# Twelve projection pieces and four gate pieces moved beside the second attention of a hybrid encoder layer; masks loaded later; the merge's PSUM pools kept and its buffers enlarged

## The chip, the cores and the metric

The kernel runs on one core of a Trainium2 chip. The core has a matrix engine (TensorE, in the profile PE, with its weight loads as PEld), VectorE (DVE), ScalarE (ACT), GpSimd (POOL), and SyncE (SP), which in this kernel only issues transfers (DMA). Each engine works through its own list of instructions in order and waits on semaphores for the others. Matrix products land in PSUM, eight banks of 128 x 512 float32; everything else is in SBUF, and larger intermediates go to DRAM and come back. The metric is the device time in microseconds (us), the median of several runs.

## What is computed

One layer of a bidirectional encoder, 2048 tokens of width 1024, float32. The tokens are also a grid of 32 rows by 64 columns.

```python
h = rms_norm(x, norm_mix)
z = h @ w_in              # q_A k_A v_A | q_B k_B v_B | gate_A gate_B
y_a = windowed_gqa(q_a, k_a, v_a, sink)       # 8 heads, |t - s| <= 128, ALiBi, sink logit
y_b = neighborhood_attn(q_b, k_b, v_b, rpb)   # 8 heads, 8 x 16 neighbours, learned bias
gates = sigmoid(concat([g_a, g_b]) + b_gate)
merged = gates[:, :D] * (y_a @ w_proj_a) + gates[:, D:] * (y_b @ w_proj_b)
x = x + merged @ w_out
x = x + square(relu(rms_norm(x, norm_mlp) @ w_up)) @ w_down
out = rms_norm(x, norm_final)
```

Every large product is made of three: each factor is split into a high and a low part (`mm3`, lines 190 to 193: high x high, high x low, low x high). So one product of 128 x 1024 by 1024 x 512 is 24 matmuls.

## The kernel before

The tokens are four blocks (`b`) of 512. The stages, with the line numbers of the profile:

1. *Input projections of blocks 0 and 1* (`in_quad`, Strassen-like, lines 412 to 438), up to line 561.
2. *Stage A, windowed attention* (`attn_a`, lines 624 to 681): 32 units, two groups of four heads times 16 blocks of 128 queries. A unit loads q, k and v (SP, lines 630 to 643), makes scores S (lines 649 and 650, PSUM tag `s`), adds the bias and takes the maximum on DVE (651), exponentiates on ACT (658), normalises on POOL (662); in its second half it transposes (668, PSUM `pt`), copies on ACT (671), subtracts on DVE (672) and multiplies with the values, PV (673 and 674, PSUM `av`). `done` collects each unit's last PV.
3. *Stage B, neighbourhood attention* (`attn_b`, lines 773 to 842): 32 units, eight heads times four column strips, in the same manner: S in line 795, maximum 799, exponential 805, normalising 809; transposes 821, copy 826, subtraction 827, PV 832. It loads qb (780 to 782), vb (786), kb (770, one per head), and for three of the four strips a bias table (763), to which POOL adds the masks (764). The masks are one tile of 128 x 3200 float32, loaded in line 747. Results go to DRAM as `y_b` through ACT's queue (`put` and `flush`).
4. *Merge* (lines 1121 to 1171): per block, products of the pages of `y_a` and `y_b` with `w_pa` and `w_pb` (PSUM `mm` and `s`), gates loaded from DRAM (`z<-zg`, 1134), sigmoid (1135), product, sum on POOL (1138), split (1139 and 1140), the product with `w_out` (PSUM `pt`), the norm, and transposes into `av` (1166). `load_y` (869 to 887) brings `y_a` and `y_b` back (`yraw`, 877) and splits them into pages.
5. *MLP*: up (from line 1180) and down (to the end), Strassen-like.

What matters here is the dense work that runs beside the attention. The input projections of blocks 2 and 3 aren't made in stage 1: `dense` (lines 722 to 727) is a list of 18 weight slices of 128 columns, k and v of A, four of q_A, and for each pair of B's heads `t` one each of k, q and v (KB, QB, VB). Each slice (`slice_of`) is a load of 512 KB, a split on ACT and POOL, and two pieces of 24 matmuls (PSUM `mm`), one for each block. The projections are stored to DRAM on SP's queue (595 and 608), in 2, 4 or 2 transfers a piece for KB, QB and VB. `gate_tile` does the same for the 16 gate slices, 32 pieces, and stores them on ACT's queue (719). So before the change 36 pieces run in stage A, and 32 gate pieces from stage B on.

The order on each engine is not written by hand: a scheduler places the instructions, with the program's order as priority. The attention stands first in the program; the dense pieces (`paced`) come after it and fill what it leaves. `paced` holds a piece back until a certain unit's PV is done:

```python
at = n * 32 // (total - rest) - lag if n < total - rest else 31
with tc.issue_after(done[at]) if at >= 0 else nullcontext():
    next(filler, None)
```

With `paced(fill, range(32), 32, 4, 4)` (line 890) the last four gate pieces wait for the last unit of B. `drive` (693 to 702) keeps two units between a unit's first half (S) and its second (PV).

Each transfer takes one of eight semaphores in turn, and its issuing engine waits until the transfer that had this semaphore before has landed.

Of the kernel before, what the change touches and what calls it, by code (L numbers as in the profile page):

```python
# [8 lines left out]
F32 = mybir.dt.float32  # L9
# [3 lines left out]
PSUM = bass.MemoryType.PSUM  # L13
# [9 lines left out]
P = 128  # L23
KC = D // P
NB = 4
# [65 lines left out]
def encoder_layer(ctx, tc, x, norm_mix, w_in, b_gate, sink, rpb, w_pa, w_pb, w_out,  # L91
# [529 lines left out]

    done = []

    def attn_a(g, i):
# [4 lines left out]
        q = T(ap_, [P, 4, P], F32R, "qa", 3)  # L629
        SY.dma_start(q.bitcast(F32), qs_a[g][i // 8][:, i % 8])  # L630
        ka = T(ap_, [P, 2, 384], F32R, "ka", 3)
# [51 lines left out]
    def chain(gens):  # L683

        now = None
        for g in gens:
            next(g)
            if now is not None:
                yield from now
            now = g  # L690
        yield from now

    def drive(units, ahead=2):

        live = []
        for u in units:
            next(u)
            live.append(u)
            if len(live) > ahead:
                next(live.pop(0), None)  # L700
        for u in live:
            next(u, None)

    def paced(filler, pieces, total, rest, lag):

        for n in pieces:
            at = n * 32 // (total - rest) - lag if n < total - rest else 31
            with tc.issue_after(done[at]) if at >= 0 else nullcontext():
                next(filler, None)

    def gate_tile(f, blocks):
        hl = slice_of([(cols(w_in[0], O_GA + f * P), KC)])
        yield
        for b in blocks:
# [5 lines left out]
            yield  # L720

    dense = [qk_tile(O_KA, 1.0), v_tile(O_VA)]
    dense += [qk_tile(O_QA + t * P, 0.125) for t in range(4)]
    for t in range(4):
        dense.append(qk_tile(O_KB + t * P, 0.125))
        dense.append(qk_tile(O_QB + t * P, 1.0, tiled=True))
        dense.append(v_tile(O_VB + t * P))
    fill = chain(dense)
    for g in range(2):
        make_bias_a(g)  # L730

    drive(attn_a(g, i) for g in range(2) for i in range(7))
    paced(fill, range(12), 36, 0, 3)
    flush()
    drive(attn_a(g, i) for g in range(2) for i in range(7, 16))
    paced(fill, range(12, 36), 36, 0, 3)
    del done[:]
# [8 lines left out]
    masks = T(bp, [P, btotal], F32, "masks", 1)  # L746
    SY.dma_start(masks, mask_b)
    jstart = {0: bstart[0], 1: bstart[2], 2: bstart[4]}
# [4 lines left out]
    def make_bias_b(h, jt):  # L753
        j = (0, 1, 3)[jt]
        w = B_W[j]
        n_bias[0] += 1
        t = T(bp, [P, 1280], F32, f"biasb{n_bias[0] % 2}", 2)
        for i in (0, 1, 3):
            n = B_NR[i] * w
            o = boff[(jt, IT[i])]  # L760
            first = h * T_ROWS * w + (B_R0[i] - 8 * i - 7 + T_RO) * w + (B_C0[j] - 16 * j - 15 + T_COFF[j])
            src = bass.AP(tabs[jt].tensor, tabs[jt].offset + first, [[w, 8], [1, 16], [1, n]])
            SY.dma_start(t[:, o : o + n], src)
        G.tensor_tensor(out=t[:, : jlen[jt]], in0=t[:, : jlen[jt]],
                        in1=masks[:, jstart[jt] : jstart[jt] + jlen[jt]], op=ALU.add)
        return t
# [94 lines left out]

    fill = chain(gate_tile(f, (2, 3)) for f in range(16))
    drive(ahead_of(all_b(), 1))
    flush()
# [4 lines left out]
    def load_y(b):  # L869
        yh, yl = [], []  # L870
        for n in range(2):
            h = T(p4, [P, 4, BT], F32R, "page", 4)
            l = T(p4, [P, 4, BT], F32R, "page", 4)
            for c in range(4):
                raw = T(p4, [P, BT], F32, "yraw", 2)
                src = (y_a[c // 2][(c % 2) * P : (c % 2 + 1) * P] if n == 0 else y_b[c])[:, b * BT : (b + 1) * BT]
                SY.dma_start(raw, src)
                hc, lc = h[:, c], l[:, c]
                if n == 1:

                    raw = flipped(raw)
                    hc, lc = (t.rearrange("p (r j c) -> p j r c", r=8, j=4) for t in (hc, lc))
                A.copy(hc, raw)
                V.tensor_tensor(out=lc, in0=raw, in1=hc.bitcast(F32), op=ALU.subtract)
            yh.append(h)
            yl.append(l)
        return yh, yl

    first_y = load_y(0)
    paced(fill, range(32), 32, 4, 4)  # L890
    s_h.close()

# [6 lines left out]
    wo = []  # L899

    s_pp.close()
    s_pp = ExitStack()
    pps.update({t: pool(f"pq_{t}", space=PSUM, stack=s_pp) for t in ("mm", "s", "pt", "av")})

# [217 lines left out]
    for b in range(NB):  # L1122
# [3 lines left out]
        for f in range(8):  # L1126
            hl = slice_of([(cols(w_pa[0], f * P), 4), (cols(w_pb[0], f * P), 4)])
            parts = []
            for n in range(2):
                ps = psum("mm" if n == 0 else "s", 2)  # L1130
                for c in range(4):
                    mm3(ps, hl[:, 0, 4 * n + c, :], hl[:, 1, 4 * n + c, :], yh[n][:, c], yl[n][:, c], c == 0, c == 3)
                g = T(wp, [P, 2, BT], F32, "z", 2)[:, 0] if n else T(p4, [P, BT], F32, "z", 2)
                SY.dma_start(g, zg[b][0][n, f * P : (f + 1) * P, :])
                A.activation(g, g, AF.Sigmoid, bias=bg[:, 8 * n + f : 8 * n + f + 1])
                V.tensor_tensor(out=g, in0=ps, in1=g, op=ALU.mult)
                parts.append(g)
# [25 lines left out]
        for k in range(KC):  # L1163
            ps = psum("av", 2)
            for t in range(4):
# [216 lines left out]
```

## Time and profile before

| | |
|---|---|
| median of 3 runs | 2761.67 us (2759.82 to 2764.2) |
| the profiled execution by itself | 2763.62 us |
| its span, first to last instruction | 2761.7 us |
| mean granted TensorE clock | 0.985 |
| busy PE | 2664.5 us, 96% of the span |
| busy DVE, ACT, POOL | 1561.0, 1244.9, 820.4 us |
| read from and written to DRAM | 342.94 and 155.26 MB |

The profile is one execution. Its page gives busy time by engine, the span in 40 slices (a digit is the busy share in tenths), the DMA queues, the chain of work that ended last, and groups of instructions by line. Views of the same trace give busy time by windows, the waits, the rows of one tile, and the instructions in order of time. A row of the latter reads: start, duration, engine, line, operation, written tile <- read tiles, and in brackets the idle time before it with what ended it. "SPq" and "ACTq" are the queues' issues of transfers. A matmul's duration overlaps the next one's.

### The profile page before, as it was taken

The numbers are of one execution on the slowest core, as the hardware profiler recorded it, in microseconds if no ns is written. First come the engines' busy times: TensorE is split into PE (matmuls) and PEld (weight loads), VectorE is DVE, ScalarE is ACT, GpSimd is POOL, SyncE is SP. The second block draws the span as 40 slices with busy tenths as digits, with TensorE's granted clock in tenths as the row PEclk, the third lists the DMA queues.
The fourth block names the chain that finished last, engine by engine and source line by source line (L and its number), as shares of the span: only waits on it lengthen the run. The fifth ranks groups of instructions, "written<-read, shape, count | busy, mean of one in ns | idle before, by whom it ended". The sixth has DMA issues, their size and how long they took to land.

```text
span 2761.7 us, 35569 instructions
## 1 busy us (share of the span) xinstructions
PE 2664.5 (96%) x12332; PEld 2196.4 (80%) x12332; DVE 1561.0 (57%) x2352; ACT 1244.9 (45%) x2227; POOL 820.4 (30%) x620
## 2 busy tenths in 40 slices
PE   7999989999989998999999999989999999999998
PEld 6887878888777787777878788878888788888887
DVE  8655455656355455533435767586654644555667
ACT  5334235555455456434433544554444332332444
POOL 1111133333354442423421355555544000000000
PEclk9999999999999998999999999999999999999999
DMA  4855276865677775646544656564434954445455
GB/s 147 229 152 190 101 230 191 221 184 158 171 205 203 202 189 157 200 131 201 181 144 171 237 167 210 186 219 149 150 137 160 331 180 160 141 153 179 171 190 173
DMA packets 348996, 500.58 MB, mean 181 GB/s; under 512 B 32505, under 2 KB 180601, under 8 KB 347665
## 3 DMA queue, kind: packets, MB, share of 16 engines
q1 hardware_dynamic: 319888, 464.74, 54.1%
q10 hardware_dynamic: 28928, 33.56, 3.6%
q8 instruction: 98, 1.61, 0.2%
q14 instruction: 82, 0.66, 0.1%
HBM read 342.94 MB, written 155.26 MB: 180 GB/s over the span
## 4 chain that ended last, share of the span: by engine, by line
PE 77%; DMA 10%; DVE 6%; issue 3%; ACT 2%; SPq 1%; POOL 0%; ACTq 0%; POOLq 0%; DVEq 0%
PE b L237 14%; PE b L239 14%; PE b L238 14%; PE mm L191 4%; PE mm L192 4%; PE mm L193 4%; PE zb L239 3%; PE zb L237 3%; PE zb L238 3%; DMA vb<-vs_b 3%; DMA z<-zg 2%; PE pt L191 1%; PE pt L192 1%; PE pt L193 1%; PE pt L668 1%
## 5 line engine op out<-in xcount | busy, mean ns | idle before, releaser
L238 PE MATMUL b<-dwh,dah 128*128 128x512 f32 x896 | 348.8, 389 | 0.0
L239 PE MATMUL b<-dwh,dah 128*128 128x512 f32 x896 | 348.0, 389 | 0.0
L237 PE MATMUL b<-dwh,dah 128*128 128x512 f32 x896 | 339.3, 391 | 2.2 <-ACT dwh L233 2.2
L230 POOL TENSOR_TENSOR uc<-uc,uc 128x512 f32<-128x512 f32 x120 | 233.5, 1961 | 221.1 <-issue 135.3
L233 ACT CAST dah<-da 128x1024 fp32r<-128x1024 f32 (+1 forms) x128 | 121.0, 945 | 366.5 <-PE b L239 243.7
L234 DVE TENSOR_TENSOR dah<-da,dah 128x1024 fp32r<-128x1024 f32 (+1 forms) x128 | 139.3, 1090 | 225.5 <-ACT dah L233 222.5
L237 PE MATMUL b<-ubh,uwhlb 128*128 128x512 f32 x592 | 231.3, 391 | 3.3 <-ACT uc L1077 1.6
L239 PE MATMUL b<-ubh,uwhlb 128*128 128x512 f32 x592 | 230.1, 391 | 2.7 <-DVE uwhlb L234 2.6
L238 PE MATMUL b<-ubh,uwhlb 128*128 128x512 f32 x592 | 231.1, 391 | 0.0
L191 PE MATMUL mm<-hT,whl 128*128 128x512 f32 x544 | 221.6, 407 | 2.3 <-DVE z L365 2.3
L230 DVE TENSOR_TENSOR uc<-b,uc 128x512 f32<-128x512 f32 x160 | 109.0, 688 | 196.4 <-PE b L239 153.4
L193 PE MATMUL mm<-hT,whl 128*128 128x512 f32 x544 | 216.8, 399 | 0.0
L192 PE MATMUL mm<-hT,whl 128*128 128x512 f32 x544 | 216.5, 398 | 0.0
L174 POOL TENSOR_TENSOR whl<-raw,whl 128x1024 fp32r<-128x1024 f32 x66 | 160.1, 2425 | 172.4 <-ACT whl L173 152.4
L237 PEld LDWEIGHTS b<-dwh,dah 128*128 128x128 f32 x896 | 168.8, 189 | 37.6 <-ACT dwh L233 2.6
L1272 POOL TENSOR_TENSOR st<-st,power 128x1 f32<-128x1 f32 x16 | 13.6, 859 | 616.0 <-DVE st L1271 615.8
L238 PEld LDWEIGHTS b<-dwh,dah 128*128 128x128 f32 x896 | 168.5, 188 | 35.0
L239 PEld LDWEIGHTS b<-dwh,dah 128*128 128x128 f32 x896 | 168.4, 188 | 35.0
L237 PE MATMUL zb<-zh,zwhl 128*128 128x512 f32 x476 | 189.8, 401 | 4.8 <-DVE zh L444 2.6
L238 PE MATMUL zb<-zh,zwhl 128*128 128x512 f32 x476 | 189.7, 399 | 1.8 <-DVE zh L234 1.8
L239 PE MATMUL zb<-zh,zwhl 128*128 128x512 f32 x476 | 187.0, 399 | 0.5 <-DVE zwhl L234 0.5
L237 PEld LDWEIGHTS b<-ubh,uwhlb 128*128 128x128 f32 x592 | 111.5, 188 | 27.1 <-ACT uc L1077 2.0
(236 smaller groups left out, 6232.4 us busy)
## 6 DMA issues: line engine op xcount, KB each, us to landing
at<-uc SPq DMA_DIRECT2D x224, 256.0 KB
da<-at SPq DMA_DIRECT2D x96, 512.0 KB
dw<-in_w_down_dram SPq DMA_DIRECT2D x160, 256.0 KB
uraw<-in_w_up_dram SPq DMA_DIRECT2D x32, 1024.0 KB
raw<-in_w_in_dram SPq DMA_DIRECT2D x34, 512.0 KB
zraw<-in_w_in_dram SPq DMA_DIRECT2D x16, 1024.0 KB
z<-zg SPq DMA_DIRECT2D x64, 256.0 KB
xin<-in_x_dram SPq DMA_DIRECT2D x16, 512.0 KB
```

The costliest lines, as they stand in the source:

```text
L174: G.tensor_tensor(out=hl[:, 1], in0=raw, in1=hl[:, 0].bitcast(F32), op=ALU.subtract)
L191: PE.matmul(ps, lh, rh, start=first, stop=False)
L192: PE.matmul(ps, lh, rl, start=False, stop=False)
L193: PE.matmul(ps, ll, rh, start=False, stop=last)
L230: return eng.tensor_tensor(out=out, in0=a, in1=b, op=op).ins
L233: A.copy(hi, src)
L234: eng.tensor_tensor(out=lo, in0=src, in1=hi.bitcast(F32), op=ALU.subtract)
L237: PE.matmul(ps, lh, rh, start=first, stop=False, skip_group_check=True)
L238: PE.matmul(ps, lh, rl, start=False, stop=False, skip_group_check=True)
L239: PE.matmul(ps, ll, rh, start=False, stop=last, skip_group_check=True)
L668: PE.transpose(pt[:, h * P : (h + 1) * P], s[:, h, c * P : (c + 1) * P], ident)
L1272: G.tensor_tensor(out=r, in0=r, in1=power, op=ALU.pow)
```

## The change

1. `dense` now runs in stage A only with its first 24 pieces (k, v, q of A, and heads 0 to 3 of B), paced over A's 32 units. The other 12 pieces (heads 4 to 7 of B) are put ahead of the 32 gate pieces in one chain, and these 44 are paced over B's 32 units, in two parts: 22 behind the first 15 units in the program's order, 22 behind the rest. The argument `rest` is gone, so that no piece is kept for after B.
2. `drive` takes its list of live units from outside and drains it only where `last` is true, so that the units of both parts are one stream.
3. `began` collects the first load of each unit of A. The load of the masks, and all loads of bias tables, are issued only after the 21st of them.
4. The merge keeps the PSUM pools of the attention instead of closing them and opening its own. `s` has three banks there instead of two, and the transposes behind the norm use one bank of `av` instead of two (in the last block three of `s`).
5. `yraw` has six buffers instead of two, the first gate tile `z` four instead of two.

```diff
-    done = []
+    done, began = [], []
...
-        SY.dma_start(q.bitcast(F32), qs_a[g][i // 8][:, i % 8])
+        began.append(SY.dma_start(q.bitcast(F32), qs_a[g][i // 8][:, i % 8]).ins)
...
-    def drive(units, ahead=2):
-
-        live = []
+    def drive(units, live, last, ahead=2):
+
         for u in units:
             next(u)
             live.append(u)
             if len(live) > ahead:
                 next(live.pop(0), None)
-        for u in live:
-            next(u, None)
-
-    def paced(filler, pieces, total, rest, lag):
+        while last and live:
+            next(live.pop(0), None)
+
+    def paced(filler, pieces, total, lag):
 
         for n in pieces:
-            at = n * 32 // (total - rest) - lag if n < total - rest else 31
+            at = n * 32 // total - lag
             with tc.issue_after(done[at]) if at >= 0 else nullcontext():
                 next(filler, None)
...
-    fill = chain(dense)
+    fill = chain(dense + [gate_tile(f, (2, 3)) for f in range(16)])
...
-    drive(attn_a(g, i) for g in range(2) for i in range(7))
-    paced(fill, range(12), 36, 0, 3)
+    live = []
+    drive((attn_a(g, i) for g in range(2) for i in range(7)), live, False)
+    paced(fill, range(12), 24, 3)
     flush()
-    drive(attn_a(g, i) for g in range(2) for i in range(7, 16))
-    paced(fill, range(12, 36), 36, 0, 3)
+    drive((attn_a(g, i) for g in range(2) for i in range(7, 16)), live, True)
+    paced(fill, range(12, 24), 24, 3)
...
-    SY.dma_start(masks, mask_b)
+    with tc.issue_after(began[20]):
+        SY.dma_start(masks, mask_b)
...
-            SY.dma_start(t[:, o : o + n], src)
+            with tc.issue_after(began[20]):
+                SY.dma_start(t[:, o : o + n], src)
...
-    fill = chain(gate_tile(f, (2, 3)) for f in range(16))
-    drive(ahead_of(all_b(), 1))
+
+    units = ahead_of(all_b(), 1)
+    drive((next(units) for _ in range(15)), live, False)
+    paced(fill, range(22), 44, 4)
+    flush()
+    drive(units, live, True)
...
-                raw = T(p4, [P, BT], F32, "yraw", 2)
+                raw = T(p4, [P, BT], F32, "yraw", 6)
...
-    paced(fill, range(32), 32, 4, 4)
+    paced(fill, range(22, 44), 44, 4)
...
-    s_pp.close()
-    s_pp = ExitStack()
-    pps.update({t: pool(f"pq_{t}", space=PSUM, stack=s_pp) for t in ("mm", "s", "pt", "av")})
...
-                ps = psum("mm" if n == 0 else "s", 2)
+                ps = psum("mm" if n == 0 else "s", 2 if n == 0 else 3)
...
-                g = T(wp, [P, 2, BT], F32, "z", 2)[:, 0] if n else T(p4, [P, BT], F32, "z", 2)
+                g = T(wp, [P, 2, BT], F32, "z", 2)[:, 0] if n else T(p4, [P, BT], F32, "z", 4)
...
-            ps = psum("av", 2)
+            ps = psum("av", 1) if b < NB - 1 else psum("s", 3)
```

## The prediction

> **What bounds the kernel now.** I read the page first, then busy time by windows, then the chain of waits of the stage that is not full, then single rows. From the page:
>
> ```profile
> span 2761.7 us, 35569 instructions
> PE   7999989999989998999999999989999999999998
> DVE  8655455656355455533435767586654644555667
> ```
>
> TensorE (PE) is the bound: most slices are at 9, while VectorE's highest is 8, in the first. A change can win only where PE waits, so I cut the slices that the change touches into stages. Columns: window, length, busy us of PE (instructions), PEld, DVE, ACT, POOL, granted clock, DMA share, GB/s.
>
> ```profile
> 395.00:735.00 340.00, 333.71 (x1688) 279.59 (x1687) 200.66 (x540) 190.17 (x475) 119.17 (x149) 0.98 0.68 187
> 735.00:800.00 65.00, 55.49 (x284) 45.81 (x283) 26.36 (x74) 29.80 (x74) 36.17 (x33) 0.97 0.70 200
> 800.00:1050.00 250.00, 231.11 (x1332) 199.43 (x1330) 134.12 (x340) 135.31 (x319) 113.79 (x115) 0.97 0.77 199
> 1050.00:1107.00 57.00, 45.87 (x255) 39.15 (x254) 31.38 (x70) 35.86 (x76) 12.04 (x18) 0.85 0.53 154
> 1107.00:1130.00 23.00, 23.00 (x101) 18.58 (x100) 2.00 (x3) 6.89 (x10) 3.38 (x2) 1.00 0.36 118
> 1130.00:1480.00 350.00, 338.53 (x1484) 270.88 (x1483) 152.26 (x178) 144.35 (x232) 126.32 (x76) 0.99 0.55 175
> ```
>
> 395 to 735 is the windowed attention ("stage A"): PE idle 6.3 of 340 us. 735 to 1107 is the neighbourhood attention ("stage B"): idle 9.5 + 18.9 + 11.1 = 39.5 us, and the clock withheld 0.03 x 65 + 0.03 x 250 + 0.15 x 57 = 18 us more. 1107 to 1130 are the four gate pieces that were kept for after B: no idle at all. Then the merge: idle 11.5, clock 3.5. So B alone leaves some 58 us, and A is full. What B waits for stands in the chain of waits from 735 to 1107:
>
> ```profile
> by line: DMA vb<-vs_b 22.8%; PE av L832 9.3%; PE mm L191 8.1%; PE mm L192 7.9%; PE mm L193 7.8%; PE pt L821 7.2%; PE s L795 6.5%; DMA raw<-in_w_in_dram 5.7%; DMA biasb<-tab 4.5%; SPq L763 3.7%; issue 2.4%; DVE plb L827 2.3%; SPq L786 2.1%;
> ```
>
> Transfers (vb, weights, bias) and their issue on SP's queue head it: a unit's PV matmuls (L832) come before its values or its softmax have. In the kernel's instruction order a steady B unit has one piece of 24 dense matmuls between its PV groups, in one lump, and PV often follows two transposes and one S matmul; little covers a late transfer or a late ACT copy.
>
> **The change, part by part.** The price of a dense matmul, from a run without a wait (first and last of 22):
>
> ```profile
> 738.09 0.40 PE L191 MATMUL mm<-hT,whl 128*128 128x512 f32 x1
> ...
> 742.97 0.40 PE L191 MATMUL mm<-hT,whl 128*128 128x512 f32 x1
> ```
>
> 21 steps in 4.88 us, 0.232 us each; a piece of 24 is 5.6 us. Twelve pieces (six weight slices) leave A: -67 us there if PE stays its bound. B gets these 12 and the four gate pieces that stood behind it (22 us): +89 us of work. The total of PE's work is unchanged, so this part is worth only what happens to the waits.
>
> *B's middle.* Visible: 18.9 + 7.5 = 26.4 us. Waits under 0.16 us do not show, since a matmul counts 0.39 us busy and the next starts after 0.232; with four PV groups in each of some 22 units (250 us of the 372 that 32 units take) that hides at most 88 x 0.16 = 14 us. So 26 to 40, I take 34. In the changed order a steady unit has some 33 dense matmuls instead of 24, in two or three groups, and most second transposes are followed by 9 to 20 dense matmuls before their PV; a unit's S-to-PV distance grows from about 79 to about 100 dense matmuls (5 us). I take two thirds as covered: **-22**, bounds 0 and -40.
>
> *B's start* (9.5 + 2.0 us). The first two units have 30 and 24 dense matmuls between S and PV, against 29 and 24 before, and the second bias table is still loaded behind stores of projections. **0**, bounds -11 and +8 (the stores, below).
>
> *B's drain* (11.1 + 8.6 us). Before, the last four units have no dense work left. Now the last gates and 42 matmuls of the merge lie among them, while the last two units stay bare: half, **-10**, bounds 0 and -20.
>
> *The cover that goes.* The four kept pieces hid the way of the last unit's result through DRAM into the merge. Rows of that way (PE's last PV, then ACT, SP, ACT):
>
> ```profile
> L832 PE MATMUL av<-plb,vb x256: 272/282/580, 758.8 to 1103.7; 96*128 96x256 f32 x64, 128*128 128x256 f32 x64
> 1104.00 0.59 ACT L839 COPY yb<-av 64x512 f32<-64x512 f32 x1 [1.24 <-PE av L832]
> 1105.33 0.53 ACTq L170 DMA_DIRECT2D y_b<-yb  x1
> 1107.98 0.33 SPq L877 DMA_DIRECT2D yraw<-y_b  x1
> 1111.07 0.62 ACT L883 CAST page<-yraw 128x512 fp32r<-128x512 f32 x1 [0.83 <-DMA yraw<-y_b]
> L884 DVE TENSOR_TENSOR page<-yraw,page x32: 675/691/1599, 1078.5 to 1396.1; 128x512 fp32r<-128x512 f32 x32
> ```
>
> From 1103.7 to 1111.7 + 0.7 are 8.7 us. In the changed order nothing stands after the last PV that does not need this result (the matmuls of s for the last heads come next), and on SP the load of yraw stands behind the fifth load of w_out, on ACT the page cast behind five casts of wo: 8.7 is the least if the order holds. With some 2 us of lowered clock after the gap, **+10.5**; bounds 0 (drain and gap overlap) and +13. The clock here: 0.85 granted in the window with PE's gaps of B's drain, 1.00 in the one behind.
>
> [...]
>
> *Masks.* They and six bias loads now wait for A's 21st unit. Before they ran between A's first loads:
>
> ```profile
> 392.35 0.41 SPq L747 DMA_DIRECT2D masks<-in_mask_b_dram  x1
> 392.81 4.56 SPq L763 DMA_DIRECT2D biasb<-tab  x4
> 397.46 2.09 SPq L630 DMA_DIRECT2D qa<-qs_a  x1
> ```
>
> The next unit's qa was issued 5 us after the masks. Later the same queue time lies beside a full A. **-4**, bounds -6 (A's visible idle) and 0.
>
> *A with less cover.* Per unit PE needs (333.7 - 67) / 32 = 8.3 us instead of 10.4; DVE 200.66 / 32 = 6.3, ACT 5.9, before the evictions that leave. PE stays the fullest, so nothing forces a loss, but S-to-PV shrinks from about 100 to 72 dense matmuls, and the second unit's PV follows the first's with none. Nearest row: B's middle, which lost 26.4 of 250 us (11%) with a similar cover; on A's 273 us that is +29, less the 13 that A shows already (6.3 idle, 6.8 clock), +16. Bounds 0 and +29, I take **+7**.
>
> *Merge.* It keeps the pools, s has three banks, z four buffers, yraw six, the transposes behind the norm one bank. Its waits sit where the next block's pages are loaded:
>
> ```profile
> 1175.00:1190.00 15.00, 11.99 (x42) 8.56 (x41) 6.75 (x8) 7.05 (x11) 6.30 (x4) 0.81 0.54 160
> 1278.00:1290.00 12.00, 7.85 (x28) 5.54 (x27) 5.28 (x8) 4.51 (x7) 4.07 (x3) 0.86 0.52 148
> 1376.00:1386.00 10.00, 7.67 (x31) 5.39 (x31) 5.81 (x8) 4.55 (x7) 4.61 (x3) 1.00 0.50 158
>   ACT page L883: 30.8, 17
> ```
>
> Idle 3.0 + 4.2 + 2.3, clock 2.9 + 1.7: 14 us. The last row is ACT's wait for yraw, 30.8 us in 17 waits with two buffers. Six buffers let the loads run ahead; the casts still follow the last use of the old page. **-8**, bounds -14 and 0. The single bank costs nothing where 12 to 24 matmuls lie between two groups of transposes, as in the changed order; uncovered, each of 24 groups would wait for ACT's 0.6 us, +14.
>
> Sum: -22 + 0 - 10 + 10.5 - 4 + 7 - 8 = **-26.5**. The profiled execution took 2763.6 us by itself (span 2761.7), so 2737.1; the median of the runs, 2761.67, is 1.9 lower, so I say **2735**.
>
> **Rivals.**
>
> *Stage B becomes paced by SP's queue (slower).* A dense piece's stores are issued on SP and wait for their eviction, with all later loads behind. In A, 395 to 735:
>
> ```profile
> SPq L608 <- DVE v L350: 17.4, 4, 6.5
> SPq L595 <- ACT z L364: 16.8, 6, 6.1
> SPq L595 <- DVE z L365: 16.6, 5, 5.8
> SPq L595 <- ACT z L360: 11.5, 6, 3.8
> ...
> L191 PE MATMUL mm<-hT,whl 128*128 128x512 f32 x283 | 114.8, 406 | 0.0
> ```
>
> 62.3 us for some 35 pieces (3 x 283 dense matmuls over 24, the last row's kind being a third of them), 1.8 each; 12 pieces bring 21 us of standing into B, 32 stores and 6 weight loads, in front of vb, qb and bias, which already lead the chain. If B follows its loads, the middle's -22 is void and 21 are added: 2735 + 43 = 2778. It decides once loads, not dense matmuls, end most PV waits. For it: vb's 22.8%. Against: by the order the moved pieces end by B's fifth unit, and the gates store through ACT. 0.17.
>
> *A falls to attention's own pace:* +29 instead of +7, 2757. For it: exp, transpose, copy and subtract follow each other on ACT and DVE. Against: 75% load of DVE. 0.11.
>
> *Everything is covered:* middle -40, drain -20, the gap behind B hidden (0): 2735 - 18 - 10 - 10.5, about 2696. For it: A before, idle 2% with 27 dense matmuls a unit. Against: the bare last units. 0.15.
>
> *The change does not do what it says:* the waits follow the units wherever dense work lies, because they end with transfers: middle and drain stay, 2735 + 32 = 2767. Against: 79 matmuls of distance shrank them to 0.1 of the stage already. 0.08.
>
> **How the numbers follow.** Forecast 0.49, with its own range 2720 to 2754. A measurement of this kernel tells 0.2% (5.5 us) from no change. Faster: forecast 0.49, all covered 0.15, half of the A case 0.06: 0.70. Slower: the queue case 0.17 and a part of the last, 0.03: 0.20. The same: the rest, 0.10. Range 2700 to 2776: it takes in the A case, the last rival and the near side of the queue case, and leaves out about a half of the "all covered" case and of the queue case.
>
> **What would show it.** Right: PE's idle in the units of B below 4% with the clock near 1; stage A about 65 us shorter with idle under 10 us more; a single PE gap of 8 to 13 us between the last PV (av) and the next merge matmul of s, ended by ACT's page cast, with a lowered clock behind it; the three block boundaries of the merge nearly without ACT waits for yraw. Wrong: DVE or ACT over 85% in A with PE below 93%; vb or SP's stores still leading B's chain with 20% or more; a merge that waits for its one av bank; or no gap behind B.

## The result and the profile after

The changed kernel takes 2757.64 us (median of 20 runs, 2753.35 to 2760.68), the kernel before 2762.92 us beside it (20 runs, 2758.09 to 2768.08). The ratio is 0.998, 95% interval 0.9973 to 0.9987: 5.5 us faster by the ratio, where 26.5 were forecast. Run again in a later group it gave 0.9978 (0.9967 to 0.9989). The sign is right and the size is a fifth of the forecast. The time lies inside the wide range of 2700 to 2776, but above the 2720 to 2754 that the prediction gave to its main line.

From the page of the changed kernel (its profiled execution took 2753.35 us by itself, 10.3 less than the profiled one before, the low end of its runs):

```profile
span 2751.6 us, 35508 instructions
PE   7999999999899999899998899989999999999998
```

A slice is 69 us. PE's row has lost its dents in the slices 6 (start of A), 12 (from B's start into its middle) and 16 (B's drain), and has new ones in 11 (B's start), 17 (the way into the merge), 22 and 23 (end of the merge, start of up). The stages by windows, columns as in the prediction:

```profile
395.00:690.00 295.00, 282.81 (x1440) 231.04 (x1439) 189.68 (x525) 177.15 (x449) 106.84 (x143) 0.99 0.68 189
690.00:800.00 110.00, 96.30 (x503) 80.83 (x502) 48.81 (x130) 50.41 (x123) 54.23 (x49) 0.95 0.82 216
800.00:1067.00 267.00, 265.52 (x1494) 229.48 (x1493) 119.33 (x312) 135.94 (x316) 115.96 (x114) 1.00 0.69 185
1067.00:1113.00 46.00, 39.89 (x231) 34.00 (x229) 24.00 (x49) 29.93 (x57) 8.54 (x10) 0.93 0.56 175
1113.00:1130.00 17.00, 5.81 (x14) 3.97 (x14) 10.41 (x11) 10.11 (x11) 2.69 (x2) 0.53 0.78 266
1130.00:1465.00 335.00, 328.82 (x1457) 266.11 (x1456) 145.63 (x175) 137.55 (x223) 120.76 (x74) 0.99 0.54 176
1465.00:1560.00 95.00, 84.30 (x365) 67.29 (x364) 57.54 (x58) 41.40 (x61) 15.20 (x10) 0.95 0.52 180
```

B's middle (800 to 1067) is full: idle 1.5 us, clock 1.00. The losses sit elsewhere: 13.7 us idle at B's start, 6.1 in B's drain, 11.2 between B's last PV and the merge, and 10.7 in the last row, a stretch that the prediction did not look at. It is the end of the merge's last block and the first matmuls of the next stage, called "up" here (lines 237 to 239). Before, that stretch was nearly full, with 2.3 us idle:

```profile
1467.00:1560.00 93.00, 90.75 (x408) 73.40 (x407) 67.03 (x68) 43.43 (x65) 10.94 (x8) 1.00 0.56 193
```

The chain of waits through B (690 to 1113) is now led by the dense matmuls; vb, 22.8% before, is gone from the head:

```profile
by line: PE mm L191 15.7%; PE mm L193 15.6%; PE mm L192 15.6%; PE av L835 11.9%; PE pt L824 9.3%; PE s L798 8.9%; DMA kb<-ks_b 4.3%; DMA ks_b<-z 2.0%; issue 1.9%; DMA qb<-qs_b 1.6%; DMA biasb<-tab 1.6%; ACT phb L829 1.2%; DMA raw<-in_w_in_d
```

PE's four longest waits between 1440 and 1560 us, with what ended them (total us, times, longest):

```profile
PE pt L191 <- DVE xr L1160: 4.4, 1, 4.4
PE s L1169 <- ACT h2s L1171: 4.3, 2, 3.7
PE b L237 <- ACT h2s L1171: 3.2, 1, 3.2
PE b L237 <- ACT ubh L233: 1.3, 1, 1.3
```

Two of the four are waits for h2s: the copies that empty the banks of the last block's transposes. One of them holds these transposes themselves ("s"), the other a matmul of "b", that is of up, not of the merge.

The way of B's last result into the merge, in order of time (start, length, engine, line, what; idle time before it in brackets):

```profile
1113.21 0.58 ACT L842 COPY yb<-av 64x512 f32<-64x512 f32 x1 [1.24 <-PE av L835]
1114.54 0.52 ACTq L170 DMA_DIRECT2D y_b<-yb  x1
...
1117.86 0.37 SPq L884 DMA_DIRECT2D yraw<-y_b  x1
...
1122.57 0.62 ACT L890 CAST page<-yraw 128x512 fp32r<-128x512 f32 x1 [0.85 <-DMA yraw<-y_b]
...
1123.24 1.22 PE L191 MATMUL s<-page,whl 128*128 128x512 f32 x2 [10.07 <-ACT page L890]
```

To compare stages I add up, from the trace, the time from each PE instruction's start to the next one's, less the usual step of an instruction of its size (the 30th percentile over the whole run); this holds idle time, a lowered clock and waits too short for the views. In us:

| stage | before | after | change | forecast terms |
|---|---|---|---|---|
| up to 395 | 32.2 | 29.2 | -3.0 | none |
| A (395 to 735; after, to 690) | 20.1 | 29.3 | +9.2 | masks -4, less cover +7 |
| B's start (to 800) | 15.0 | 24.9 | +9.9 | 0 |
| B's middle (to 1067) | 41.4 | 12.3 | -29.1 | -22 |
| B's drain and the way into the merge (to 1135) | 21.6 | 26.9 | +5.3 | -10, +10.5 |
| merge (to 1465) | 24.1 | 15.3 | -8.8 | -8 |
| its end, start of up (to 1560) | 4.6 | 16.2 | +11.6 | none |
| the rest | 16.0 | 10.9 | -5.1 | none |

The column of changes adds up to -10.0, the two profiled executions' own difference; 8.1 of it lie in the first and the last row, ahead of and behind everything that was priced. A second profile of the changed kernel (x9) gives 29.5, 26.1, 11.7, 26.1, 15.9 and 16.9 in the stages from A to up, so a change of 2 us in one of them says nothing.

### The profile page after: what moved, and what is told of

Its sections match the earlier page's. It is cut to its first block, busy times and chain, and to the rows that moved or that the text cites. A ratio compares the mean times of both kernels' runs of the same rounds, so it can differ in the third digit from the quotient of the medians.

```text
span 2751.6 us, 35508 instructions
## 1 busy us (share of the span) xinstructions
PE 2654.0 (96%) x12332; PEld 2186.5 (79%) x12332; DVE 1546.3 (56%) x2352; ACT 1243.4 (45%) x2227; POOL 821.1 (30%) x620
## 4 chain that ended last, share of the span: by engine, by line
PE 86%; DMA 5%; DVE 4%; ACT 2%; issue 2%; POOL 1%; SPq 1%; ACTq 0%; POOLq 0%; DVEq 0%
PE b L237 14%; PE b L239 14%; PE b L238 14%; PE mm L191 5%; PE mm L192 5%; PE mm L193 5%; PE zb L237 4%; PE zb L238 4%; PE zb L239 4%; PE pt L191 2%; PE pt L192 2%; PE pt L193 2%; PE av L835 2%; PE pt L824 1%; PE s L798 1%
## 5 line engine op out<-in xcount | busy, mean ns | idle before, releaser
L239 PEld LDWEIGHTS b<-dwh,dah 128*128 128x128 f32 x896 | 168.2, 188 | 34.9
L802 DVE CUSTOM_DVE_ANT_0 sb<-s,biasb 128x384 f32<-128x384 f32 (+2 forms) x128 | 68.8, 562 | 127.6 <-PE pt L824 92.3
```

Source lines behind the costliest of these rows:

```text
L239: PE.matmul(ps, ll, rh, start=False, stop=last, skip_group_check=True)
L802: V.tensor_tensor_reduce(out=si[:, :n], in0=ps[:, :n], in1=bias[:, o : o + n], scale=1.0, scalar=-3.0e38, op0=ALU.add, op1=ALU.max, accum_ ...
```

## The experiments

Runs of one group shared a chip and the runs of the kernel before. The ratio is to the kernel before; 0.001 is 2.8 us; the changed kernel stands at 0.998 (0.9973 to 0.9987). Two runs whose intervals overlap are not told apart by their times. The stages are the table's, in us of loss, from one profiled execution each. In the expectations "causal attention" is stage A, "junction" the way into the merge, and "the planner" the scheduler.

| run | median us | ratio (95%) | A | start | middle | drain, way | merge | up |
|---|---|---|---|---|---|---|---|---|
| x1 one bank of av | 2752.41 | 0.9968 (0.9956 to 0.998) | 30.1 | 23.0 | 12.2 | 27.6 | 15.2 | 9.3 |
| x2 pools reopened | 2746.12 | 0.9945 (0.993 to 0.9961) | 30.2 | 24.1 | 11.9 | 27.6 | 11.8 | 5.4 |
| x3 up's banks in another order | 2748.75 | 0.9955 (0.9941 to 0.9969) | 29.9 | 24.8 | 12.9 | 27.5 | 15.1 | 7.7 |
| x4 four pieces held | 2751.35 | 0.9961 (0.9947 to 0.9975) | 30.0 | 18.7 | 22.4 | 14.7 | 16.8 | 16.0 |
| x5 masks early | 2753.82 | 0.9956 (0.9943 to 0.997) | 34.9 | 25.6 | 11.5 | 25.8 | 15.6 | 12.3 |
| x6 old buffers | 2764.86 | 1.0 (0.9992 to 1.0008) | 31.4 | 23.9 | 14.6 | 27.3 | 21.8 | 17.9 |
| x7 the move alone | 2765.0 | 1.0 (0.9991 to 1.0009) | 34.1 | 24.4 | 12.2 | 27.8 | 26.4 | 5.0 |
| x8 x2 and x4 | 2738.32 | 0.9903 (0.9888 to 0.9918) | 31.7 | 17.8 | 23.5 | 16.7 | 16.7 | 5.4 |
| x9 the changed kernel again | 2758.1 | 0.9978 (0.9967 to 0.9989) | 29.5 | 26.1 | 11.7 | 26.1 | 15.9 | 16.9 |
| x10 masks early again | 2755.6 | 0.9966 (0.9955 to 0.9976) | 34.7 | 25.6 | 12.3 | 25.1 | 15.1 | 12.1 |
| x11 x8 and masks early | 2746.55 | 0.9937 (0.9919 to 0.9955) | 34.4 | 20.9 | 20.2 | 18.0 | 17.1 | 5.6 |
| x12 x8 and y_b stored by SP | 2733.2 | 0.9888 (0.987 to 0.9905) | 28.3 | 16.3 | 23.7 | 12.1 | 16.7 | 5.2 |
| x13 y_b stored by SP | 2749.8 | 0.9948 (0.9935 to 0.9961) | 31.6 | 18.2 | 13.7 | 28.4 | 15.3 | 16.1 |
| x14 second bias added later | 2739.71 | 0.9917 (0.9904 to 0.993) | 28.0 | 19.5 | 10.7 | 25.6 | 12.1 | 10.0 |
| x15 x12 and x14 | 2734.54 | 0.9894 (0.9882 to 0.9907) | 28.4 | 17.3 | 23.1 | 11.3 | 16.3 | 5.2 |

### The start of up: x1, x2, x3

The first quad of up takes its eight banks in the order of the old pools: mm has 0 and 1, and s has 2, 3, 4 in the changed kernel. Its second tile pair (n = 5) takes banks 2 and 3, where the last block's transposes now are.

x1:

```diff
-            ps = psum("av", 1) if b < NB - 1 else psum("s", 3)
+            ps = psum("av", 1)
```

> The changed kernel, but in the merge's last block the transposes go through the one bank av, as in the other blocks, instead of through the three banks of s. My theory: about 16 us are lost after 1465 us because the first quad of up wants the banks 2 and 3 (n = 5), which are banks of s and wait for the last block's transposes and their copies; with av (bank 7, which no tile of the first quad uses) most of it comes back, 10 to 16 us against the changed kernel: about 2742 to 2748, and the waits of b and s on ACT h2s at 1500 to 1520 go. Rival (the norm itself is late, the bank is not the cause): 2755 to 2762. Rival on the other side (eight transposes through one bank, each behind its copy, hold PE up): 2760 to 2770.

x2:

```diff
+    s_pp.close()
+    s_pp = ExitStack()
+    pps.update({t: pool(f"pq_{t}", space=PSUM, stack=s_pp) for t in ("mm", "s", "pt", "av")})
...
-                ps = psum("mm" if n == 0 else "s", 2 if n == 0 else 3)
+                ps = psum("mm" if n == 0 else "s", 2)
...
-            ps = psum("av", 1) if b < NB - 1 else psum("s", 3)
+            ps = psum("av", 2)
```

> The changed kernel with one part undone: the merge's own PSUM pools of two banks each are opened again, its transposes use two banks of av in every block, one tile of a block less in s. My theory: the loss at the start of up (16 us) comes back, 10 to 16 us, and the block boundaries stay covered, since these hang on yraw and z buffers; reopening the pools costs at most 2 us at the first page matmul: about 2742 to 2749. Rival (keeping the banks was worth what I forecast for it, at the merge's start): 2755 to 2762, with the gap after the last PV of the neighbourhood attention longer by 3 us or more.

x3:

```diff
     pms.extend(pool(f"pm{i}", space=PSUM) for i in range(8))
+    pms[:] = [pms[i] for i in (0, 1, 5, 6, 7, 2, 3, 4)]
```

> The changed kernel, its transposes of the last block still in the three banks of s, but the eight banks of up are taken in another order: mm, pt, av and then s, so that of the first quad only the fourth pair is on s. My theory: it gets back part of the 16 us, 5 to 12: about 2746 to 2753, with the matmuls of n = 5 ahead of the transposes. Rival (transposes or norm late by themselves): 2755 to 2760.

The reopened pools give back 9.7 us against the changed kernel (0.9945 to 0.998), and the whole stretch is as before. Its row and all of PE's waits from 1440 to 1560 in x2:

```profile
1465.00:1560.00 95.00, 91.91 (x413) 74.31 (x413) 66.59 (x64) 43.60 (x65) 22.97 (x14) 1.00 0.53 182
```
```profile
PE b L237 <- ACT uc L1084: 1.6, 1, 1.6
PE b L237 <- ACT uwhlb L233: 0.7, 1, 0.7
PE b L237 <- DVE uc L230: 0.7, 1, 0.7
PE pt L191 <- DVE xr L1164: 0.5, 1, 0.5
```

No wait for h2s is left. The 4.4 us wait for xr at 1453 has gone too (0.5); it is 0.5 also in x6, which keeps the pools and their banks, so the kept banks alone do not make it. x3 touches neither the transposes nor their banks, only which banks up asks for first, and gets 6.9 us back: so it is the banks, not a late norm, that hold up. It does not remove the whole loss. Its two waits for h2s in the same window:

```profile
PE b L237 <- ACT h2s L1171: 3.2, 1, 3.2
PE s L1169 <- ACT h2s L1171: 0.4, 1, 0.4
```

The transposes hardly wait any more; up itself still waits once for the last copies. x1 gets back half in the trace (16.2 to 9.3) and 3.3 us by its ratio, below what was expected and with an interval that overlaps the changed kernel's: with one bank of av up runs ahead, but the transposes queue behind their own copies instead (PE av on ACT h2s 2.1 us, PE b on ACT h2s 0.8).

### The way into the merge: x4, x8

```diff
-    def paced(filler, pieces, total, lag):
+    def paced(filler, pieces, total, lag, rest=0):
...
-            at = n * 32 // total - lag
+            at = n * 32 // (total - rest) - lag if n < total - rest else 31
...
-    paced(fill, range(22), 44, 4)
+    paced(fill, range(22), 44, 4, 4)
...
-    paced(fill, range(22, 44), 44, 4)
+    paced(fill, range(22, 44), 44, 4, 4)
```

> The changed kernel, but the last four gate pieces (24 matmuls of 512 columns each, some 22 us in all) wait until the neighbourhood attention's last PV, as they did before, and the other forty are paced over its 32 units. My theory: they fill the 10.3 us gap between the last PV and the first page matmul, and the lowered clock behind it goes: 8 to 14 us less than the changed kernel: 2743 to 2750. Rival A (the attention's middle loses its cover: 40 pieces where 44 just covered it): 2753 to 2760, with the middle's PE share under 48 of 50. Rival B (the held pieces keep the page matmuls waiting, and ACT, which must copy their gates, makes the page casts later): 2755 to 2765.

> The two edits that gained alone, together: the merge's own PSUM pools opened again (-9.7 us against the changed kernel by its ratio) and the last four gate pieces held until after the last PV (-5.2 by its ratio). My theory: they lie at different places (1465 to 1560 and 690 to 1135 us) and add: 2740 to 2745. Rival (the held pieces run into the reopening of the pools, and what one gains the other gives back): 2746 to 2752.

In x4 a gate's matmul follows the last PV at once, where the changed kernel has 10.07 us of idle time:

```profile
1088.49 0.27 PE L835 MATMUL av<-plb,vb 96*128 96x128 f32 x1
1088.60 0.44 PE L191 MATMUL mm<-hT,whl 128*128 128x512 f32 x1
```

Drain and way fall from 26.9 to 14.7, the start from 24.9 to 18.7, the middle rises from 12.3 to 22.4 (rival A in part: four pieces fewer do uncover it, though PE is still busy for 260.2 of its 267 us). Why the start gains is not tested. Net 5.2 us by the ratios, under the 8 expected, with intervals that just touch. Together with x2 in x8 the gain is 21 us by the ratios, where 9.7 and 5.2 were to be added; in the traces the stages from A to up lose 13 us less than in the changed kernel, each where it did in the single runs. So the two add; that they do more than add is not shown. x8 beats both kernels: 26.8 us under the kernel before.

### Buffers, and the move alone: x6, x7

x6:

```diff
-                raw = T(p4, [P, BT], F32, "yraw", 6)
+                raw = T(p4, [P, BT], F32, "yraw", 2)
...
-                g = T(wp, [P, 2, BT], F32, "z", 2)[:, 0] if n else T(p4, [P, BT], F32, "z", 4)
+                g = T(wp, [P, 2, BT], F32, "z", 2)[:, 0] if n else T(p4, [P, BT], F32, "z", 2)
```

> The changed kernel with two buffers each of yraw and z in the merge, as before. My theory: the waits of the page casts for yraw at the three block boundaries come back, 6 to 10 us between 1135 and 1465 us, the sum's merge term: 2763 to 2769. Rival (the boundaries are covered by the dense order, not by buffers): 2755 to 2760.

x7 is x2, x5 and x6 in one, so that only the move of the pieces is left.

> Part one alone: the projections of heads 4 to 7 and the gates are spread over both attentions as in the changed kernel; masks load early, the merge opens its own pools, its buffers are the old ones. My theory, from the losses of the two traces: middle of the neighbourhood attention -29, its start +10, the causal attention +9, drain and junction +6, start of up 0, boundaries as before: 2757 to 2762, about the kernel before. Rival (the start's +10 is the late masks'): 2748 to 2755. Rival (the move gains its whole 22 to 29, the rest of the change gives it back): 2738 to 2745.

x6: the merge's loss goes from 15.3 to 21.8 and the time by 5.5 us (1.0 to 0.998), as expected. ACT's waits for yraw in the merge, x6 first, then the changed kernel:

```profile
ACT page L890 <- DMA yraw<-y_b: 15.3, 7, 3.0
ACT page L890 <- DMA yraw<-y_a: 5.8, 4, 3.0
```
```profile
ACT page L890 <- DMA yraw<-y_b: 4.7, 5, 2.0
```

x7 takes as long as the kernel before (1.0, 0.9991 to 1.0009), a little over what was expected: what the middle gains (41.4 to 12.2) A (+14.0), the start (+9.4) and drain and way (+6.2) give back. So the move of the pieces, for which the terms of the prediction add up to -14.5 (-22, 0, -10, +10.5, +7), was worth nothing.

### Masks: x5, x9, x10, x11

```diff
-    with tc.issue_after(began[20]):
-        SY.dma_start(masks, mask_b)
+    SY.dma_start(masks, mask_b)
...
-            with tc.issue_after(began[20]):
-                SY.dma_start(t[:, o : o + n], src)
+            SY.dma_start(t[:, o : o + n], src)
```

> The changed kernel, but masks and the first biases load when the planner likes, as before, not behind the twentieth unit of the causal attention. My theory: late masks cost or gain little in themselves (-4 forecast), but loading them late puts 13 bias and mask loads into the start of the neighbourhood attention, where the DMA share is 0.85 and 10 us were lost that I forecast as nothing; with early loads the first POOL additions (L767, 702 us and on) come before its first units and the losses between 690 and 800 us fall by 4 to 10 us: about 2748 to 2755. Rival (the late loads are worth the 4 us forecast): 2759 to 2765, lost between 380 and 650 us. Rival (neither): 2755 to 2759.

> The changed kernel once more, as the partner of the three runs beside it on one chip. By its ratio of 0.998 to the kernel before: 5 us less than it, 3 to 8. Both theories on the masks want this number from the same chip.

> The changed kernel with early masks once more, beside the changed kernel. Its first timing was 6 us better than the changed kernel by the two ratios, its trace says 2 us worse: 400 to 450 us lose 6 us more (PE busy 39 of 50 against 45), the attention's start is the same. Theory by the trace: 2 to 7 us slower than the run beside it, and the late masks earn their 4 us. Theory by the first timing: 4 to 8 us faster than the run beside it.

> Pools opened again, four gate pieces held, and masks early. Without the last edit the ratio to the kernel before was 0.9903 (27 us). Theory by the trace (late masks are good for 4 to 6 us): ratio 0.9915 to 0.993. Theory by the first timing of early masks: ratio 0.987 to 0.9885.

x5's number fitted my theory and its reason did not: the start did not move (25.6). The first 55 us of A, x9 with late masks, then x10 with early ones, on the same chip:

```profile
395.00:450.00 55.00, 51.77 (x262) 41.67 (x261) 39.50 (x118) 37.97 (x103) 23.46 (x35) 0.97 0.65 190
```
```profile
395.00:450.00 55.00, 45.20 (x220) 36.62 (x220) 37.88 (x102) 33.46 (x95) 24.59 (x32) 0.91 0.74 218
```

Late masks save 6.6 us of idle time there. Yet x10 was 2.5 us faster than x9, with overlapping intervals: neither expectation. The start of up took it back (16.9 against 12.1). The last block's transposes stand in another order there, some among the wo matmuls, where the changed kernel has nine in one run behind the last of them; presumably the scheduler's order moved with the loads that the edit set free 1000 us earlier. With the pools reopened that stretch no longer varies (5.4 and 5.6 in x8 and x11), and late masks are worth 9 us by the ratios (0.9937 to 0.9903; they come from two groups, and their intervals just do not meet), more than the theory by the trace said, and some 4 in the traces of the two.

### The start of B: x12, x13, x14, x15

ACT's waits from 690 to 800 us in the changed kernel; the engine stands in front of a DMA issue of its own, mostly a store of y_b (line 170), which waits until the transfer that had its semaphore before has landed (the store issued at 785.14 us has the semaphore of a load of biasb that was issued at 778.42 and landed at 785.06):

```profile
ACT phb L829 <- DMA biasb<-tab: 9.6, 1, 9.6
ACT phb L829 <- DMA ks_b<-z: 7.1, 1, 7.1
ACT sb L808 <- DVE stb L805: 6.7, 4, 3.6
ACT z L364 <- DMA kb<-ks_b: 5.6, 1, 5.6
ACT z L605 <- DMA qb<-qs_b: 5.1, 1, 5.1
ACT z L605 <- DMA qs_b<-z: 4.5, 1, 4.5
```

Five waits for landings, 31.9 us in 110, where the kernel before had 4.4 in the 65 us of its start (735 to 800). At the end of four of the five ACT issues a store of y_b. Meanwhile PE waits for ACT's casts of phb:

```profile
PE av L835 <- ACT phb L829: 8.7, 3, 4.7
```

What such a wait costs when the engine also has casts to do stands in ACT's rows, 9.63 us between two casts of phb:

```profile
775.53 0.59 ACT L829 CAST phb<-pt 128x512 fp32r<-128x512 f32 x1
785.14 0.52 ACTq L170 DMA_DIRECT2D y_b<-yb  x1
785.75 0.59 ACT L829 CAST phb<-pt 128x512 fp32r<-128x512 f32 x1 [9.63 <-DMA biasb<-tab]
```

x13 is this edit on the changed kernel, x12 the same edit on x8:

```diff
-        put(y_b[t].rearrange("(e d) (i j t) -> e d i j t", e=2, i=4, j=4)[e, :, :, j, :],
-            y.rearrange("d (i t) -> d i t", i=4))
+        SY.dma_start(y_b[t].rearrange("(e d) (i j t) -> e d i j t", e=2, i=4, j=4)[e, :, :, j, :],
+                     y.rearrange("d (i t) -> d i t", i=4))
```

> Pools opened again, four gate pieces held, and the stores of y_b issued by SP in place of ACT. In the changed kernel ACT sits some 30 us between 690 and 1100 us behind DMA issues that wait for a landing, and PE waits 10 us for its casts of phb, most of it at the start of the neighbourhood attention. Theory (these issues cause the loss of 10 us at the start): PE's waits for ACT phb fall under 4 us and the time by 4 to 8: ratio 0.9875 to 0.989. Rival (the wait moves to SP's queue and delays q, v and the biases): ratio 0.990 to 0.995, waits of PE for DVE or DMA in their place.

> The changed kernel with one edit: the stores of y_b are issued by SP in place of ACT. Theory (ACT held behind its own stores is a cause of the 10 us lost at the start of the neighbourhood attention, against a forecast of 0): the loss between 690 and 800 us falls from 25 to 15 to 20 us and the ratio to the kernel before from 0.998 to 0.9945 to 0.9965. Rival (its 5 us in the combined kernel came from the drain or the junction only): the start loses 23 to 27 us as before, the stretch 1067 to 1135 us less.

In x13 one of ACT's waits for a landing is left, and PE's waits for phb are gone. ACT's row, and PE's longest in the same 110 us:

```profile
ACT v L349 <- DMA vs_b<-v: 8.8, 1, 8.8
```
```profile
PE mm L191 <- DVE v L350: 5.0, 1, 5.0
```

The start's loss falls from 24.9 to 18.2, the time by 8.8 us (0.998 to 0.9948), both as expected; 5.0 us of what is left are a new wait behind that one landing. The profiled execution was the slowest of x13's six, and its other stages from A to up lose some 5 us more than the changed kernel's, so its trace bears out 6.7 us in the start and not the 8.8 of the whole. In x12, with the pieces held, the same edit is worth 4.1 us by the ratios, whose intervals overlap, and in the traces it acts mostly in A (31.7 to 28.3) and in drain and way (16.7 to 12.1), not in the start. x12 has the lowest ratio of the study, 30.9 us under the kernel before; x15 lies within its interval.

x14 moves POOL's addition of the second bias. Changed kernel, then x14:

```profile
702.00 2.91 POOL L767 TENSOR_TENSOR biasb<-biasb,masks 128x1280 f32<-128x1280 f32 x1 [8.94 <-DMA qb<-qs_b]
704.89 2.11 POOL L812 TENSOR_SCALAR sb<-sb,stb 128x288 f32<-128x288 f32 x4
```
```profile
698.51 2.11 POOL L822 TENSOR_SCALAR sb<-sb,stb 128x288 f32<-128x288 f32 x4 [3.77 <-DVE stb L819]
703.20 2.93 POOL L775 TENSOR_TENSOR biasb<-biasb,masks 128x1280 f32<-128x1280 f32 x1 [2.58 <-DMA qb<-qs_b]
```

```diff
-        G.tensor_tensor(out=t[:, : jlen[jt]], in0=t[:, : jlen[jt]],
-                        in1=masks[:, jstart[jt] : jstart[jt] + jlen[jt]], op=ALU.add)
-        return t
+        return [t, False]
+    norms = []
+    def added(b, jt):
+        t = b[0]
+        if not b[1]:
+            with tc.issue_after(norms[max(len(norms) - 2, 0)]) if norms else nullcontext():
+                G.tensor_tensor(out=t[:, : jlen[jt]], in0=t[:, : jlen[jt]],
+                                in1=masks[:, jstart[jt] : jstart[jt] + jlen[jt]], op=ALU.add)
+            b[1] = True
+        return t
...
         yield
+        bias = added(bias, jt)
...
-            G.tensor_scalar(s[i][:, :n], s[i][:, :n], ri[:, i : i + 1], 1.0, ALU.mult, ALU.mult)
+            norm = G.tensor_scalar(s[i][:, :n], s[i][:, :n], ri[:, i : i + 1], 1.0, ALU.mult, ALU.mult).ins
+        norms.append(norm)
```

> The changed kernel with one edit: POOL adds the mask to the second bias behind the first unit's normalisation instead of ahead of it. In the changed kernel POOL waits 9 us (to 702 us) for loads of that bias that SP issues at 693 us and later, and the first unit's normalised scores queue behind it. Theory (this queue costs part of the start's 10 us): the first PV comes 4 to 7 us earlier, the loss between 690 and 800 us falls by 2 to 6 us: ratio 0.996 to 0.9975. Rival (the wait only moves to the second unit, whose scores need that bias): ratio 0.9975 to 0.999, a wait of like size some 8 us later.

> Pools opened again, four gate pieces held, y_b stored by SP, and the bias edit. Without the bias edit the ratio was 0.9888, with a gap of 7.9 us ahead of the first transposes at 698 us. Theory: that gap falls under 3 us and the ratio to 0.9865 to 0.988. Rival (the gap moves to the second unit): 0.988 to 0.990.

The first unit's normalisation runs 6.4 us earlier, and the start loses 19.5 instead of 24.9, as expected; the first PV comes only 2.8 us earlier (705.6 against 708.4), where 4 to 7 were expected. PE's 8.7 us of waits for phb are gone here as well, although ACT still issues the stores and waits 28.4 us for landings in the start. So x13 and x14 remove in part the same loss, and their gains are not to be added up. The ratio of 0.9917 is far better than 5.4 us account for: merge (15.3 to 12.1) and start of up (16.2 to 10.0), which the edit does not touch, came out in a better order. In x15, where that place is settled, the gap of 7.8 us ahead of the first transposes is gone as expected, but the edit gains nothing (0.9894 against 0.9888), as the rival said. Its first PV comes 9.3 us earlier than x12's (700.9 against 710.2) and its last PV 0.8 later (1083.5 against 1082.7): what the start gains, the rest of B gives back. So the price of x14's edit by itself stays open; 0 to 5 us is what these runs bear out.

## Why the prediction was wrong

The forecast was -26.5; the stages that it priced came to -1.9 in the traces (-29.1 + 9.9 + 5.3 + 9.2 - 8.8 and the 11.6 that was not priced), and the times give -5.5. Against the traces the sum was 24.6 too good. Three of its terms failed: the merge term left out the hand-over of the banks to the next stage, B's start was put at nothing without a price for its queues, and A's thinner cover was halved without a reason. Step by step:

- **The merge term, 11.6 of it.** "It keeps the pools, s has three banks": the term priced the block boundaries and the 24 groups of transposes in the one bank of av, and did not ask who owns the banks of s after the merge. The last block's eight groups go to s, whose banks up wants second. x2 and x3 show it: the loss goes with the pools (16.2 to 5.4), and for the greater part with up's order of banks alone (to 7.7). The rest of the term was right: -8 forecast, -8.8 in the traces, and x6 puts the buffers at 5.5 us. The single bank of av cost nothing in the first three blocks: between 1135 and 1465 us PE has no wait for the copies behind it.
- **B's start, 9.9.** Priced at 0 with bounds of -11 and +8, by counting dense matmuls between S and PV. What came was a wait that cover by dense work does not reach: ACT behind its stores (x13, 6.7 us of loss) and POOL's queue behind a bias that lands late (x14, 5.4 of loss). The two overlap, and how the 9.9 divide between them stays open. The prediction named the second, "loaded behind stores of projections", and gave it no price. It named the moved pieces' stores for SP's queue only; in B the landings of their stores and of the loads around them (ks_b, qs_b, kb, qb, biasb) are those for which ACT's own issues wait. That these landings come later than before is not shown.
- **A with less cover and masks, 6.2.** Masks were right in their stage: -4 with bounds of -6 and 0, 5.2 us of loss (x9 against x10); in the time of the changed kernel they do not show (x5 and x10), in that of x8 they do (x11). So A's thinner cover cost some 14 (9.2 + 5.2, and +14.0 in x7), not 7; the nearest row that I had, B's middle, gave +16 after what A showed already, and I halved it without a reason. What the views show of it are short waits in front of PV: PE waits 4.4 us for ACT's copies (0.8 before) and 2.5 for DVE's last sum of a unit, ya (0.8 before). A's span shrank by 50 us (last PV 737.9 to 687.6), not by 65: A loses 9.2 us more, and PE has only 248 instructions fewer in its window (1688 to 1440), not the 288 of the twelve pieces.
- **Drain and way, 4.8.** Of the 26.9 us, 10.3 are the gap behind the last PV and 4.7 what follows it to 1135; some 12 stay for the drain, against 21 before. So the drain's -10 came as -9. The way's order held step by step, but its price was 15 instead of 10.5: 8.7 was called the least, and the lowered clock behind it lasted longer. No run shows the some 2 us that the term has for that clock; behind this gap it came to 3.1 in the changed kernel, at a granted clock of 0.50 until 1131.2.
- **B's middle, 7.1 the other way.** -22 forecast, -29.1 measured, inside the bounds. Here PE's idle is 0.6% and the clock 1.00, and vb is out of the chain's head. Over all of B (690 to 1113) the sign named, idle under 4%, did not come: 21.3 of 423 us, 5.0%.

None of the rivals took place as a whole; the one with A at attention's own pace had the right place, at twice the size. Its 2757 us match the result by chance: it asked for +29 in A, and A's cost was half of that. Nor does the right sign speak for the forecast's largest terms: the move is worth 0 in x7, the buffers gave 5.5 us (x6), and the kept pools cost 9.7 (x2).

Part of the 11.6 is not a matter of banks alone. Edits far away move the start of up by 4 to 6 us (x5, x10, x14), so each single run's price carries the scheduler's order elsewhere; the prices above rest on the stage where the edit acts, and the ratio is given beside them.

## What to carry to other kernels

When a kernel keeps PSUM banks over a stage boundary, look at which tile of the next stage takes each bank first, and in what order; a bank that is the last to be emptied should be the last to be asked for (here 6.9 us by the times, x3). Work moved under a stage covers its matmuls, not its queues: count what each engine issues there, and try to keep stores off an engine whose casts the PE waits for (here 8.8 us by the times, 6.7 in the start's trace). Where all dense work is spread evenly, keep some of it (here four pieces, 22 us, which cut drain and way from 26.9 to 14.7 and gave back 10 in the middle) to cover the way from a stage's last result into the next. And price a move on the stage that loses its cover as carefully as on the one that gains it.

## What the runs showed of the hardware

This is about the clock after a wait. Behind the 4.35 us wait at 1453 in the changed kernel, the first slow matmuls, the last and the next one:

```profile
1457.73 0.79 PE L191 MATMUL pt<-wo,mh 128*128 128x512 f32 x1 [4.35 <-DVE xr L1160]
1458.32 0.63 PE L192 MATMUL pt<-wo,mh 128*128 128x512 f32 x1
1458.75 0.63 PE L193 MATMUL pt<-wo,ml 128*128 128x512 f32 x1
...
1462.16 0.47 PE L192 MATMUL pt<-wo,mh 128*128 128x512 f32 x1
1462.47 0.39 PE L193 MATMUL pt<-wo,ml 128*128 128x512 f32 x1
```

For 4.5 us the steps were 0.427 us (1458.32 to 1458.75) instead of 0.232, which costs 2.1 us over the wait itself. Behind the gap at 1113, a second wait of 1.12 us fell into the slow stretch, and the slow matmuls went on from 1123.24 to 1131.2, 8 us:

```profile
1127.29 0.80 PE L191 MATMUL mm<-page,whl 128*128 128x512 f32 x1 [1.12 <-ACT whl L173]
...
1130.87 0.57 PE L193 MATMUL mm<-page,whl 128*128 128x512 f32 x1
1131.27 0.39 PE L191 MATMUL mm<-page,whl 128*128 128x512 f32 x1
```

By windows the granted clock was 0.50 from 1455.49 to 1462.32, 6.8 us that begin within the wait, and 1.00 from there to 1470. Around the gap it was 1.00 from 1104 to 1114.16, 0.50 from there to 1131.23, 17.1 us, and 1.00 from there to 1140. The matmuls ran at the slower step (0.427 against 0.232) for 4.5 us of the first stretch, and for the 8 of the second, in which the work was broken once. By these rows a gap's extra is 2.1 us, and 3.1 in the broken case (6.9 us of slow work x 0.195 / 0.427). Whether the second wait is what lengthened the stretch is not tested.
